# A hybrid decoder block on one core: within an attention head, the next head's maxima earlier and the head's own scores later

## The chip, the core and the metric

The kernel runs on one core of a Trainium2 chip. TensorE (PE) multiplies matrices and writes into PSUM; VectorE (DVE) and ScalarE (ACT) read PSUM and the on-chip memory SBUF; GpSimd (POOL) works on SBUF and issues some of the transfers; SyncE (SP) only issues transfers (DMA). Each engine runs its own queue of instructions in order and waits for others by semaphores. The metric is the device time of one execution in microseconds (us), as the median of several; lower is better.

## The reference

One decoder block over 1024 tokens of width 1024, all in float32. Two groups of eight attention heads read the same normalised input. Group B (forgetting attention) adds cumulated log forget gates as a bias; group A lets each query attend to the 256 keys that an indexer scores highest, with a linear distance bias (ALiBi). Then come an output projection and a mixture of 32 experts, of which each token uses two. What the change touches is the attention:

```python
def forgetting_attention(q, k, v, log_f):
    ...
        logits = jnp.einsum('bqhd,bshd->bhqs', qb, k).astype(jnp.float32) * scale
        logits = logits + jnp.transpose(cb, (0, 2, 1))[..., None] - cum_k[:, :, None, :]
        ...
        p = jax.nn.softmax(logits, axis=-1).astype(v.dtype)
        o = jnp.einsum('bhqs,bshd->bqhd', p, v)
...
def dsa_attention(q, k, v, iq, ik, iw):
    ...
        _, idx = lax.top_k(score, n_top)
        ...
        logits = logits - slopes[None, None, :, :, None] * dist[:, :, None, None, :]
        logits = jnp.where(valid[:, :, None, None, :], logits, -jnp.inf)
        p = jax.nn.softmax(logits, axis=-1).astype(v.dtype)
```

## The kernel before

The sixteen heads run one after the other in a loop (line 1091) of 17 stages. Heads 0 to 7 are group B, 8 to 15 group A. Stage n mixes the steps of three heads:

- **scores of head n** (`score_steps`): twelve blocks, for two halves of 512 queries and each block of 128 keys up to them. A block forms the product of keys and queries in PSUM (`pst`) in two parts (`kx` by `qx`, then `ky` by `qy`, the low-order parts) plus a third product for the mask (`diagT` in group B, `maskT` in group A). ACT takes the exponential into `P`.
- **values of head n-1** (`value_steps`): twelve products of `P` with the values, collected in `po`. Each is two matmul records in the trace.
- **maxima of head n+1** (`max_steps`): for eight blocks of 128 queries the row `qx` by `kx` is formed in `pmax`, and DVE takes the largest logit of each query into `mx`. Then `finish` turns `mx` on PE (`pmt`), ACT copies it negated into `mr`, and SP copies `mr` into a row of `qx` of head n+1, so that the scores come out with the maximum already taken off. The scores of head n+1 need that copy.

There are two sets of operand tiles `qx, kx, qy, ky`, for even and odd heads (in the order of the instructions their numbers are 2764 to 2767 for even heads and 2876 to 2879 for odd ones). `prep(n + 2)` reloads the set of head n for head n+2: SP copies the queries into `qx` (from `QB` or `QA`), clears the row of the maxima (`qx<-qx`), copies the keys into `kx` (from `KB`; for heads 8 and 9 from `KA`; for heads 10 to 15 they stay), then `qy` and `ky`; POOL copies the rows of the gates (`CU`) or the slopes (`sl`). All of these must wait until head n's last scores have read the set, and head n+2's maxima must wait for them.

What else runs in a stage comes from `side(n)`: the search for the 256th largest index score (stages 0 to 3), the masks (4 to 7), sums of the adaLN vectors (in stages 8, 10, 12 and 14 POOL loads eight tiles `wada` of 512 KB, and DVE adds them up), squares and their column sums for the norms (`osq`, `psqc`).

`merge` sets the order: each list of steps is spread over a stretch of the stage, from `lo` to `hi` as shares of the stage, in proportion to each step's cost, and single steps have a place of their own. The steps are then sorted by place and issued; PE keeps that order. A scheduler orders the other engines' queues by when it expects each instruction to be ready.

```python
            todo.append((lo + (hi - lo) * (t + 0.5 * c) / tot, k, f))
    ...
    for _, _, f in sorted(todo, key=lambda z: z[:2]):
```

Of the kernel before, what the change touches and what calls it, by code (L numbers as in the profile page):

```python
# [38 lines left out]
def hymba_block(ctx: ExitStack, tc: tile.TileContext, x, c, w_ada, b_ada, g_mix, w_in, b_forget,  # L39
# [13 lines left out]
    def u(name, dt=F32, shape=(128, 1024)):  # L53
        return upool.tile(list(shape), dt, name=name, tag="u", bufs=NU)
# [13 lines left out]
    def mm(*a, **k):  # L68
        i = tc.keep_in_program_order(T.matmul(*a, **k))  # L69
        at["pe"] = i  # L70
        return i
# [9 lines left out]
    def ps1(name, shape=(128, 512), dt=F32):  # L81
        return psum.tile(list(shape), dt, name=name, tag="p", bufs=4)
# [653 lines left out]
    def max_steps(n):  # L736
        par, masked = n % 2, n >= 8
        e = E0[par]
        mx = []

        def rows(i):
            if not mx:
                mx.append(sm("mx", [128, 8]))
            w_ = (i + 1) * 128
            p = ps2("pmax")
            plain = masked and i >= 2
            for n0 in range(0, w_, 512):
                m = min(512, w_ - n0)
                last = n0 + m == w_
                mm(p[:, n0:n0 + m], qx[par][:, i * 128:(i + 1) * 128], kx[par][:, n0:n0 + m],  # L750
                   start=True, stop=plain or not last)
                if last and not plain:
                    mm(p[:, i * 128:w_], identb, diag, start=False, stop=True)
            if plain:
                V.tensor_tensor_reduce(mjunk[:, :w_], p[:, :w_], madd[i], 1.0, NEG, OP.add, OP.max,  # L755
                                       accum_out=mx[0][:, i:i + 1])
            else:
                V.tensor_reduce(mx[0][:, i:i + 1], p[:, :w_], AX.X, OP.max)  # L758

        def finish():  # L760
            p = ps1("pmt2")
            tr(p[0:8, 0:128], mx[0], identf)
            mr = sm("mr", [8, 128], F32R, bufs=1)
            S.activation(mr, p[0:8, 0:128], AF.Copy, scale=-1.0)
            cp(qx[par][e + 4:e + 5], mr)

        return [((i + 1) * 0.11 + 0.2, lambda i=i: rows(i)) for i in range(NT)], finish

    def score_steps(n, P):

        par, masked = n % 2, n >= 8
        tl = {}

        def block(hf, kb):
            q0 = max(kb * 128, hf * 512)
            m = (hf + 1) * 512 - q0
            p = ps1("pst")
            free = not masked and q0 != kb * 128
            mm(p[:, :m], kx[par][:, kb * 128:(kb + 1) * 128], qx[par][:, q0:q0 + m], start=True, stop=False)
            mm(p[:, :m], ky[par][:, kb * 128:(kb + 1) * 128], qy[par][:, q0:q0 + m], start=False, stop=free)  # L780
            if masked:
                mm(p[:, :m], identb, maskT[kb][:, q0:q0 + m], start=False, stop=True)
            elif not free:
                mm(p[:, :128], identb, diagT, start=False, stop=True)
            if hf == 0:
                slot = (0, 0), (0, 512), (1, 0), (0, 896)
            else:
                slot = (0, 0), (0, 512), (1, 0), (1, 512), (2, 0), (2, 512), (3, 0), (2, 896)
            i, off = slot[kb]
            if (hf, i) not in tl:  # L790
                tl[hf, i] = u("P")
            P[hf, kb] = tl[hf, i][:, off:off + m], q0
            S.activation(P[hf, kb][0], p[:, :m], AF.Exp)  # L793

        return [((hf + 1) * 512 - max(kb * 128, hf * 512), lambda hf=hf, kb=kb: block(hf, kb))
                for hf in range(2) for kb in range(4 * hf + 4)]
# [8 lines left out]
    def value_steps(n, P):  # L805

        j, par = (n % 8) // 2, n % 2
        g, blk, h = (1, 1 + j, 2 * j + par) if n < 8 else (0, 0, j + 4 * par)
        z, row = h // 2, MAIN[h % 2]
        cols = slice(0, 128) if par == 0 else slice(64, 192)  # L810
        po = {}

        def step(hf, kb):
            if kb == 0:
                po[hf] = ps1("po")
                if (g, hf, z // 2) not in O:
                    O[g, hf, z // 2] = u(f"O{g}{hf}", shape=(128, 2, 512))
                if (g, z) not in DEN:
                    DEN[g, z] = u("den")
            pt, q0 = P[hf, kb]  # L820
            mm(po[hf][:, q0 - hf * 512:], vblock(blk, kb)[:, cols], pt, start=(kb == 0), stop=(kb == 4 * hf + 3))
            if kb == 4 * hf + 3:
                S.activation(DEN[g, z][row, hf * 512:(hf + 1) * 512], po[hf][OTHER[par]], AF.Copy)
                S.activation(otile(g, hf, z)[row], po[hf][MAIN[par]], AF.Copy)

        return [((hf + 1) * 512 - max(kb * 128, hf * 512), lambda hf=hf, kb=kb: step(hf, kb))
                for hf in range(2) for kb in range(4 * hf + 4)]

    def normalise(g, z):

        den = DEN[g, z]
        st = {}

        def guess():
            st["r"] = r = u("rden")
            paced(S.activation(r, den, AF.Ln))
            S.activation(r, r, AF.Exp, scale=-1.0)

        def one():
            paced(V.tensor_tensor(den, den, st["r"], op=OP.mult))  # L840

        def two():
            paced(V.scalar_tensor_tensor(st["r"], den, 2.0, st["r"], op0=OP.subtract, op1=OP.mult))

        def times(hf):
            o = otile(g, hf, z)
            paced(V.scalar_tensor_tensor(o, o, -1.0, st["r"][:, hf * 512:(hf + 1) * 512], op0=OP.mult, op1=OP.mult))

        return [guess, one, two, lambda: times(0), lambda: times(1)]
# [44 lines left out]
    def prep(n):  # L894

        j, par = (n % 8) // 2, n % 2
        e = E0[par]
        if n < 8:
            h = 2 * j + par
            fill_q(par, QB[j])  # L900
            fill_k(par, KB[j])
            cp(qx[par][e + 2:e + 3], CU[96 + h:97 + h], G)
            cp(qx[par][e + 3:e + 4], CU[64 + h:65 + h], G)
            cp(kx[par][e:e + 1], CU[32 + h:33 + h], G)
            cp(kx[par][e + 1:e + 2], CU[h:h + 1], G)
            fill_cross(par, QB[j], KB[j])
        else:
            if n < 10:
                fill_k(par, KA)
                paced(G.memset(kx[par][e:e + 2].bitcast(F32), 0.0))  # L910
                cp(kx[par][e + 2:e + 3], held["pos"][0:1], G)
            h = j + 4 * par
            sl = held["sl"]
            fill_q(par, QA[j])
            cp(qx[par][e + 2:e + 3], sl[h:h + 1], G)
            cp(qx[par][e + 3:e + 4], sl[32 + h:33 + h], G)
            fill_cross(par, QA[j], KA if n < 10 else None)
# [147 lines left out]
    for m in range(4):  # L1065
        if m == 2:
            rows, finish = max_steps(0)
            rows = [f for _, f in rows]
# [18 lines left out]
    if True:  # L1087
        PP = {}
        norm = []
        NW = (0.2, 0.66, 0.73, 0.8, 0.87)  # L1090
        for n in range(17):
            streams = []
            if n < 16:
                PP[n] = {}
                streams.append(((0.07, 0.65) if n else (0.25, 0.85), score_steps(n, PP[n])))
            if n:
                streams.append(((0, 1), value_steps(n - 1, PP[n - 1])))
            if n + 1 < 16:
                rows, finish = max_steps(n + 1)
                streams.append(((0.15, 0.65) if n else (0, 0.5), rows))  # L1100
            extra = side(n)
            if n + 1 < 16:
                extra.append((0.75, finish))
            if n + 2 < 16:
                extra.append((0.79 if n else 0.9, lambda n=n: prep(n + 2)))
            if norm:
                extra += zip(NW if n < 16 else (0.1, 0.2, 0.25, 0.3, 0.35), normalise(*norm.pop()))
            merge(streams, extra)
            if n and n <= 8 and (n - 1) % 2:
                norm.append((1, (n - 1) // 2))  # L1110
            if n - 1 in (10, 11, 14, 15):
                norm.append((0, {10: 0, 11: 2, 14: 1, 15: 3}[n - 1]))
        for f in normalise(*norm.pop()):
            f()
# [315 lines left out]
    for i in range(NT):  # L1430
# [11 lines left out]
        if i in (5, 7):  # L1442
            i0, n = {5: (0, 4), 7: (4, 2)}[i]
# [310 lines left out]
    with tc.If(most > 128):  # L1754
# [58 lines left out]
        rows = u("ovri", I32, (128, 2, 16))  # L1813
# [85 lines left out]
```

## Time and profile before

| | us |
|---|---|
| median of 3 runs (1204.28 to 1205.78) | 1204.99 |
| the profiled execution | 1199.19 |
| its span, first to last instruction | 1197.2 |
| PE busy (88% of the span) | 1055.7 |
| DVE busy (77%) | 919.0 |
| ACT busy (56%) | 670.0 |
| POOL busy (25%) | 300.3 |

The heads stand between some 362 and 697 us of the span. Times of instructions and waits are of the profiled execution, 5.8 us below the median. A matmul's recorded end is modelled, and the next one may start before it; a wait is the idle time of the engine ahead of an instruction, put down to the semaphore that came last.

### The profile page before, as it was taken

How to read it: one execution, taken by the hardware profiler on the slowest of the kernel's cores; microseconds unless marked ns; L12 is line 12 of the kernel's file. 1: busy time of each engine (PE TensorE's matmuls, PEld its weight loads, DVE VectorE, ACT ScalarE, POOL GpSimd, SP SyncE). 2: the span in 40 equal slices, each digit the busy share in tenths (PEclk: the TensorE clock that was granted, in tenths of full speed). 3: DMA queues.
4: the chain of work that ended last, by engine and by line, in shares of the span. 5: the costliest groups of instructions: out<-in, count | busy, mean ns of one | idle time of the engine just before them, and what ended most of it. 6: DMA issues, size and time to landing. Idle time of an engine off the chain costs nothing.

```text
span 1197.2 us, 15378 instructions
## 1 busy us (share of the span) xinstructions
PE 1055.7 (88%) x4983; PEld 796.5 (67%) x4983; DVE 919.0 (77%) x1785; ACT 670.0 (56%) x1177; POOL 300.3 (25%) x253
## 2 busy tenths in 40 slices
PE   2789999699988998998989999975999999889881
PEld 2678899588865555654656678864777777666650
DVE  5946568899976589566578665795999999888847
ACT  7544666764546545654554622334777777656635
POOL 0341031212040110213212212551222222333223
PEclk9699999899998999999999999986999999999986
DMA  8510102243463433556336634776999999999946
GB/s 345 164 36 1 41 20 65 106 150 114 149 169 89 108 81 81 133 142 195 115 87 198 245 123 141 247 251 216 311 342 320 308 314 308 317 317 315 321 117 247
DMA packets 91414, 219.94 MB, mean 184 GB/s; under 512 B 30516, under 2 KB 40932, under 8 KB 91328
## 3 DMA queue, kind: packets, MB, share of 16 engines
q1 hardware_dynamic: 75776, 185.23, 46.5%
q0 software_dynamic: 15552, 33.66, 10.3%
q8 instruction: 42, 0.69, 0.2%
q14 instruction: 44, 0.36, 0.1%
HBM read 192.43 MB, written 42.99 MB: 197 GB/s over the span
## 4 chain that ended last, share of the span: by engine, by line
PE 49%; DVE 24%; DMA 16%; ACT 5%; issue 3%; SPq 1%; POOL 1%; DVEq 0%; ACTq 0%; POOLq 0%
PE pgu L69 10%; PE py L69 6%; PE pst L69 6%; DVE mjunk L460 6%; PE po L69 6%; PE pout L69 5%; DMA raw<-in_w_gate_dram 4%; DMA raw<-in_w_down_dram 4%; PE pp L285 3%; PE pmax L69 3%; PE pvv L407 2%; DMA qx<-mr 2%; PE pxt L74 2%; ACT sjunk L464 1%; DMA raw<-in_w_up_dram 1%
## 5 line engine op out<-in xcount | busy, mean ns | idle before, releaser
L69 PE MATMUL po<-P,VT 128*128 128x512 f32 (+3 forms) x384 | 148.3, 499 | 0.3 <-ACT P L793 0.3
L793 ACT ACTIVATE P<-pst 128x512 f32<-128x512 f32 x192 | 90.9, 489 | 95.1 <-PE pst L69 93.2
L1570 POOL DMA_INDIRECT x2d<-y,tab x31 | 59.3, 1912 | 204.9 <-DVE wgu1l L1492 46.1
L69 PE MATMUL pst<-qx,kx 128*128 128x512 f32 x192 | 94.3, 491 | 13.3 <-DMA qx<-mr 11.2
L758 DVE TENSOR_REDUCE mx<-pmax 128x1 f32<-128x128 f32 (+3 forms) x80 | 52.7, 674 | 44.6 <-PE pmax L69 44.2
L69 PE MATMUL py<-raw,af 128*128 128x512 f32 x128 | 69.2, 623 | 14.3 <-DMA raw<-in_w_down_dram 14.3
L69 PEld LDWEIGHTS po<-P,VT 128*128 128x128 f32 x384 | 66.1, 195 | 18.0 <-issue 9.8
L69 PE MATMUL pmax<-kx,qx 128*128 128x512 f32 (+1 forms) x192 | 68.1, 420 | 6.4 <-DMA kx<-KB 2.0
L69 PE MATMUL py<-wd0h,ahl 128*128 128x512 f32 x128 | 67.9, 530 | 2.4 <-ACT wd0h L1491 1.9
L69 PE MATMUL pst<-qy,ky 128*128 128x512 f32 x192 | 67.6, 352 | 0.0
L358 DVE SCALAR_TENSOR_TENSOR score<-relu,iw,score 128x384 f32<-128x384 f32 (+5 forms) x42 | 43.1, 1026 | 26.7 <-ACT relu L353 23.7
L69 PEld LDWEIGHTS pst<-qx,kx 128*128 128x128 f32 x192 | 37.9, 197 | 34.2 <-issue 20.8
L285 PE MATMUL pp<-hh,wbh 128*128 128x512 f32 x128 | 51.2, 400 | 9.3 <-DVE pjl L634 9.3
L755 DVE CUSTOM_DVE_ANT_0 mjunk<-pmax,madd 128x384 bf16<-128x384 f32 (+5 forms) x48 | 42.6, 888 | 20.6 <-PE pmax L69 20.5
L69 PE MATMUL pout<-woh,oh 128*128 128x512 f32 x128 | 52.2, 408 | 2.4 <-DVE ssq L871 2.4
L460 DVE TENSOR_SCALAR_CACHE_REDUCE mjunk<-k,low 128x768 bf16<-128x768 uint16 (+1 forms) x64 | 51.8, 810 | 1.5
L1482 POOL DMA_INDIRECT xg<-h2d,tab x32 | 39.0, 1218 | 49.6 <-PE pxt L74 35.2
L1492 DVE TENSOR_TENSOR wgu2l<-raw,wgu2h 128x512 fp32r<-128x512 f32 x64 | 43.8, 685 | 9.7 <-ACT wgu2h L1491 9.6
L285 PE MATMUL pp<-hl,wbh 128*128 128x512 f32 x128 | 50.9, 398 | 0.0
L69 PE MATMUL pout<-woh,ol 128*128 128x512 f32 x128 | 50.8, 397 | 0.0
L285 PE MATMUL pp<-hh,wbl 128*128 128x512 f32 x128 | 50.8, 397 | 0.0
L69 PE MATMUL pout<-wol,oh 128*128 128x512 f32 x128 | 50.4, 394 | 0.0
(430 smaller groups left out, 3263.1 us busy)
## 6 DMA issues: line engine op xcount, KB each, us to landing
raw<-in_w_gate_dram SPq DMA_DIRECT2D x64, 512.0 KB
raw<-in_w_up_dram SPq DMA_DIRECT2D x64, 512.0 KB
raw<-in_w_down_dram SPq DMA_DIRECT2D x64, 512.0 KB
wada<-in_w_ada_dram POOLq DMA_DIRECT2D x32, 512.0 KB, 5.5
x<-in_x_dram SPq DMA_DIRECT2D x16, 512.0 KB
wada<-in_w_ada_dram SPq DMA_DIRECT2D x16, 512.0 KB
wbr<-in_w_in_dram SPq DMA_DIRECT2D x8, 512.0 KB
qy<-QB SPq DMA_DIRECT2D x16, 256.0 KB
```

The lines of the kernel that those rows point to most:

```text
L69: i = tc.keep_in_program_order(T.matmul(*a, **k))
L74: i = tc.keep_in_program_order(T.transpose(*a))
L285: at["mm"] = T.matmul(p[:, :n], w(k, a), hT[b][k][:, n0:n0 + n], start=(i == 0), stop=(i == 23))
L358: last = V.scalar_tensor_tensor(score[i], r, wv, score[i], op0=OP.mult, op1=OP.add)
L407: at["mm"] = T.matmul(p[:, :ng], hT[a][k][:, t * 128:(t + 1) * 128], parts[k // kk][b][:, k % kk, :], start=(i == 0), stop=(i == 23))
L460: paced(V.tensor_scalar(mjunk[:, :(i + 1) * 128], src, thr, None, op0=op, op1=OP.add, accum_out=self.col(self.cnt, i)))
L755: V.tensor_tensor_reduce(mjunk[:, :w_], p[:, :w_], madd[i], 1.0, NEG, OP.add, OP.max, accum_out=mx[0][:, i:i + 1])
L758: V.tensor_reduce(mx[0][:, i:i + 1], p[:, :w_], AX.X, OP.max)
L793: S.activation(P[hf, kb][0], p[:, :m], AF.Exp)
L1482: return ko(G.indirect_dma_start(out=XG[e], out_offset=None, in_=h2d, in_offset=bass.IndirectOffsetOnAxis(ap=tab[:, e:e + 1], axis=0), bou ...
L1492: ko(V.tensor_tensor(lo, w, hi.bitcast(F32), op=OP.subtract))
L1570: return G.indirect_dma_start(out=x2d, out_offset=bass.IndirectOffsetOnAxis(ap=at_, axis=0), in_=y, in_offset=None, bounds_check=L - 1, oo ...
```

## The change

Three places in the loop over stages. The scores of a stage go from 0.07 to 0.65 of it to 0.17 to 0.76; the next head's maxima from 0.15 to 0.65 to 0.09 to 0.58; their transposition and transfer from 0.75 to 0.68. Stage 0 keeps its places, and `prep` stays at 0.79 everywhere.

```diff
             if n < 16:
                 PP[n] = {}
-                streams.append(((0.07, 0.65) if n else (0.25, 0.85), score_steps(n, PP[n])))
+                streams.append(((0.17, 0.76) if n else (0.25, 0.85), score_steps(n, PP[n])))
             if n:
                 streams.append(((0, 1), value_steps(n - 1, PP[n - 1])))
             if n + 1 < 16:
                 rows, finish = max_steps(n + 1)
-                streams.append(((0.15, 0.65) if n else (0, 0.5), rows))
+                streams.append(((0.09, 0.58) if n else (0, 0.5), rows))
             extra = side(n)
             if n + 1 < 16:
-                extra.append((0.75, finish))
+                extra.append((0.68 if n else 0.75, finish))
             if n + 2 < 16:
                 extra.append((0.79 if n else 0.9, lambda n=n: prep(n + 2)))
```

PE at the boundary from head 2 to head 3, before: the last score block of head 2, a value step, the transposition of head 3's maxima, five value steps, and head 3's first scores.

```order
L69 MATMUL pst<-qx_2764,kx_2765 128x128
L69 MATMUL pst<-qy_2766,ky_2767 128x128
L69 LDWEIGHTS identb
L69 MATMUL pst<-diagT,identb 128x128
L69 MATMUL po<-P,VT_647 128x512
L74 MATMUL pmt_3407<-identf,mx 8x128
L69 MATMUL po<-P,VT_647 128x512
L69 MATMUL po<-P,VT_647 128x384
L69 MATMUL po<-P,VT_647 128x256
L69 MATMUL po<-P,VT_649 128x128
L69 MATMUL po<-P,VT_649 128x512
L69 MATMUL pst<-qx_2876,kx_2877 128x512
```

PE there now: the last of the three score blocks of head 2 that follow the transposition of head 3's maxima, five value steps, and the first maxima product of head 4.

```order
L69 MATMUL pst<-qx_2764,kx_2765 128x128
L69 MATMUL pst<-qy_2766,ky_2767 128x128
L69 LDWEIGHTS identb
L69 MATMUL pst<-diagT,identb 128x128
L69 MATMUL po<-P,VT_647 128x512
L69 MATMUL po<-P,VT_647 128x384
L69 MATMUL po<-P,VT_647 128x256
L69 MATMUL po<-P,VT_649 128x128
L69 MATMUL po<-P,VT_649 128x512
L69 MATMUL pmax<-kx_2765,qx_2764 128x128
L69 LDWEIGHTS identb
L69 MATMUL pmax<-diag,identb 128x128
```

The transposition moved ahead of the last three score blocks, and head 4's first maxima, which read the reloaded set 2764 and 2765, took the place of head 3's first scores behind the five value steps.

SP at the end of that head, before: the reload of the even set for head 4 (`QB_2135` and `KB_2328` are where its queries and keys come from) begins ahead of the copy of head 3's maxima into the odd set.

```order
L718 DMA qx_2764<-QB_2135 64x1024
L718 DMA qx_2876<-mr 1x8x128
L718 DMA qx_2764<-qx_2764 1x16x64
L718 DMA kx_2765<-KB_2328 64x1024
L718 DMA qy_2766<-QB_2135 64x1024 x2
```

SP there now.

```order
L718 DMA qx_2876<-mr 1x8x128
L718 DMA qx_2764<-QB_2135 64x1024
L718 DMA qx_2764<-qx_2764 1x16x64
L718 DMA kx_2765<-KB_2328 64x1024
L718 DMA qy_2766<-QB_2135 64x1024 x2
```

The copy of the maxima now leads, and the four reloads follow each other. At the end of head 0 the order is as it was: the reload of `qx` for head 2 first, then the copy of head 1's maxima.

POOL in stage 8, where the slope rows of head 10 stand between loads for the adaLN sums, before.

```order
L718 DMA qx_2876<-sl 1x16x64 x2
L1036 DMA wada<-in_w_ada_dram 128x1024 x5
L718 DMA qx_2764<-sl 1x16x64
L1036 DMA wada<-in_w_ada_dram 128x1024 x2
L718 DMA qx_2764<-sl 1x16x64
L1036 DMA wada<-in_w_ada_dram 128x1024
```

POOL there now.

```order
L718 DMA qx_2876<-sl 1x16x64 x2
L1036 DMA wada<-in_w_ada_dram 128x1024 x6
L718 DMA qx_2764<-sl 1x16x64
L1036 DMA wada<-in_w_ada_dram 128x1024
L718 DMA qx_2764<-sl 1x16x64
L1036 DMA wada<-in_w_ada_dram 128x1024
```

One load moved ahead of the first slope row. In stages 10 and 12 the rows of heads 12 and 14 stand as here: a row, a load, a row.

## Rows read from the trace of the kernel before

**Rows 1.** The stretch of the heads: length, then busy us (instructions) by engine, clock.

```profile
core 0: us, PE busy (x) PEld busy (x) DVE busy (x) ACT busy (x) POOL busy (x), PEclk, DMA share, GB/s
361.72:653.21 291.49, 267.16 (x1227) 167.00 (x1226) 205.70 (x361) 154.50 (x305) 54.41 (x91) 0.98 0.45 122
```

**Rows 2.** PE's waits from 369 to 660 us: total us, times, longest.

```profile
PE pst L69 <- DMA qx<-mr: 11.2, 8, 2.9
PE pmt L74 <- DVE mx L758: 2.6, 2, 1.4
PE pmt L74 <- DVE mx L755: 2.3, 2, 1.5
PE pmax L69 <- DMA kx<-KB: 2.0, 4, 0.6
PE pst L69 <- ACT osq L863: 1.4, 1, 1.4
PE pmax L69 <- DVE mx L758: 1.3, 3, 0.8
```

**Rows 3.** Timeline, end of head 2: start, length, engine, what, [wait <- releaser].

```profile
405.59 0.31 PE L69 MATMUL pst<-qx,kx 128*128 128x128 f32 x1
...
405.91 1.08 PE L69 MATMUL po<-P,VT 128*128 128x512 f32 x2
...
405.93 0.44 SPq L718 DMA_DIRECT2D qx<-QB  x1
...
408.35 0.27 PE L74 MATMUL pmt<-identf,mx 128*8 128x128 f32 x1 [1.36 <-DVE mx L758]
...
408.46 3.18 PE L69 MATMUL po<-P,VT 128*128 128x512 f32 x10
...
408.95 0.69 SPq L718 DMA_DIRECT2D qx<-mr  x1
409.68 0.54 SPq L718 DMA_DIRECT2D qx<-qx  x1
410.27 0.58 SPq L718 DMA_DIRECT2D kx<-KB  x1
...
413.93 0.30 PE L69 MATMUL pmax<-kx,qx 128*128 128x128 f32 x1 [0.64 <-DMA kx<-KB]
```

**Rows 4.** Timeline, end of head 1: the reload of kx and its reader.

```profile
391.22 0.58 SPq L718 DMA_DIRECT2D kx<-KB  x1
...
395.31 0.30 PE L69 MATMUL pmax<-kx,qx 128*128 128x128 f32 x1 [0.59 <-DMA kx<-KB]
```

**Rows 5.** Timeline, end of head 0.

```profile
369.06 1.13 PE L69 MATMUL po<-P,VT 128*128 128x512 f32 x2
...
370.95 0.58 SPq L718 DMA_DIRECT2D kx<-KB  x1
...
373.10 0.76 PE L69 MATMUL pst<-qx,kx 128*128 128x512 f32 x1 [2.91 <-DMA qx<-mr]
```

**Rows 6.** Timeline, end of head 8: slope row, adaLN load, head 9's first scores.

```profile
516.65 0.30 PE L69 MATMUL pst<-qx,kx 128*128 128x128 f32 x1
...
517.25 0.50 POOL L718 DMA_DIRECT2D qx<-sl  x1 [13.07 <-PE pst L69]
517.75 0.55 POOL L1036 DMA_DIRECT2D wada<-in_w_ada_dram  x1
...
523.74 0.47 PE L69 MATMUL pst<-qx,kx 128*128 128x512 f32 x1 [2.31 <-DMA qx<-mr]
```

**Rows 7.** Transfers into qx whose landing is recorded, from issue to landing.

```profile
DMA to landing us min/median/max: 2.9/3.5/5.1
```

**Rows 8.** Timeline, end of stage 11: the column sums.

```profile
586.00 1.84 PE L69 MATMUL psqc<-ones,osq 128*128 128x1 f32 x16
```

**Rows 9.** Busy time and granted clock of three stretches, columns as in rows 1.

```profile
372.50:379.30 6.80, 6.20 (x21) 4.43 (x21) 2.67 (x11) 1.47 (x3) 0.00 (x0) 0.50 0.83 189
466.05:484.50 18.45, 17.27 (x80) 10.38 (x78) 18.29 (x29) 8.77 (x18) 3.49 (x8) 1.00 0.40 89
608.00:611.40 3.40, 3.40 (x11) 1.98 (x9) 1.28 (x1) 1.59 (x3) 0.00 (x0) 0.51 0.83 181
```

## The prediction

> **What bounds the kernel now.** I first took the busy time of the whole stretch of heads, then the list of what TensorE (PE) waited for in it, then the timeline of single boundaries between two heads. In the 291.49 us from the first scores of head 0 to those of head 15, PE works 267.16 us; VectorE (DVE) works 205.70 and ScalarE (ACT) 154.50 [rows 1]. PE runs its instructions in the order of the code, so the time is PE's work plus what it waits for, and a reordering can only change the waits. The list names them [rows 2]: 11.2 us in 8 waits of a head's first scores for the copy of its negated maxima (qx<-mr), 2.6 + 2.3 us of the transposition of the maxima (pmt) for the last maximum on DVE, 2.0 us of the first maxima product (pmax) for the reload of kx, 1.4 us for an ACT queue that is blocked by osq, 1.3 us of pmax for DVE.
>
> The timeline of the boundary from head 2 to head 3 shows why [rows 3]. The last scores of head 2 start at 405.59. They free qx and kx, so SP issues the reload for head 4 at 405.93. PE goes on with a value step (1.08 us), waits 1.36 us for the maximum and transposes at 408.35. The copy of mr is issued at 408.95, and only behind it, in SP's order, come qx<-qx (409.68) and kx<-KB (410.27). PE covers all this with five value steps, 3.18 us long, and two score blocks; at 413.93 pmax of head 4 still waits 0.64 us for kx. So two chains end at PE after every head: maxima, mr, first scores; and last scores, reload, first maxima.
>
> **The change part by part.** *What goes.* PE's order now is: pmt, three score blocks, five value steps, two maxima, value, maximum, and only then the next head's first scores. From pmt to those scores there are then at least 3.18 us of values plus three score blocks and four products; the mr copy was waited for at most 2.9 us beyond the 3.18 us of values. I take all 11.2 us as gone. Before pmt there now stand two 512-wide score blocks and a value step where two narrow blocks and a value step stood, and a further value step; the added step alone is 1.08 us [rows 3], against waits of 1.4 and 1.5 us at most: I take the 4.9 us as gone, too. The 2.0 us for kx are replaced by what follows. Sum: 18.1 us.
>
> *What comes.* The reload still waits for the head's last scores, but the next maxima come sooner after them. Cover: from the last scores' start to the next step 0.32 us (405.59 to 405.91), then the five value steps, 3.18 us: 3.50 us. Chain: 0.34 us to the first issue, two issues of 0.44 and 0.54 us with their gaps of about 0.05 (kx comes 0.59 after qx<-qx), so kx is issued 1.42 us after the last scores, since mr no longer stands between. From the issue of kx to the maxima that it released it took 3.66 us (410.27 to 413.93) [rows 3] and 4.09 (391.22 to 395.31) [rows 4]; I take 3.9. So the maxima can start 5.3 us after the last scores, and PE waits 5.3 - 3.5 = **1.8 us** (1.6 to 2.0) for each of heads 3 to 9, whose kx is reloaded: 12.6 us.
>
> Head 2 stands apart: at the end of head 0 SP's order is not changed, and in PE's order only one value step stands between the last scores and head 2's maxima. That step ends at 369.06 + 1.13 = 370.19; kx is issued at 370.95 and lets the maxima start at 374.85: **4.7 us**, where PE waited 2.91 for mr before (counted above) [rows 5].
>
> Heads 10 to 15 keep kx; their last piece is the second slope row (qx<-sl) on POOL's queue. Into heads 10, 12 and 14 the change puts one adaLN load (wada) between the two rows, where two stood at head 10. First row 0.60 us after the last scores, row 0.50, load 0.55 [rows 6], landing 3.5 us after its issue (median; 2.9 to 5.1) [rows 7]: 5.15 us, less 3.5: **1.65 us**, three times 5.0. Into heads 11, 13 and 15 no load stands between: 0.60 + 0.50 + 3.5 = 4.6, a wait of **1.1 us**, but head 13's maxima stand behind sixteen column sums of 1.84 us [rows 8] that cover it: 2.2 us. New waits in all: 4.7 + 12.6 + 5.0 + 2.2 = **24.5 us**.
>
> *What the new waits give back.* While PE stands, ACT and DVE catch up: the osq wait and DVE's 1.3 us before pmax lie just behind the new wait, and I count them as absorbed, 2.7 us (0 to 2.7). The granted clock was 0.50 (1.2 GHz) in two stretches [rows 9]: for 6.8 us after the 2.91 us wait at head 1, and for 3.4 us from 608.0, where PE worked throughout. The second costs 1.7 us and goes, if no wait as long as those before it follows; in the first PE worked 6.20 us at half clock, lost 3.1, and would start 1.75 us later, losing 2.2. Together 2.6 us.
>
> *Sum:* -18.1 - 2.7 - 2.6 + 24.5 = **+1.1 us**. The profiled execution took 1199.19 us (span 1197.2 and 2 us around it), 5.8 below the median of the runs, 1204.99; I add the difference to the median: **1206.1 us**, +0.1%. Under 0.2% (2.4 us) no measurement of this kernel tells a difference from no change. Its own range: with 3.66, 2.9 and 2.9 us for the three landings it is 4.7 us less, 1201.4; with 4.09 us for kx (+1.3), nothing absorbed (+2.7) and one half-clock stretch more (+1.7) it is 1212, of which I take 1211.
>
> The Trainium skill ("DMA: Bandwidth & Descriptors", Anatomy of one DMA) gives a transfer some 2.0 us fixed and then 436 GB/s, for GpSimd's path; by an estimate from that page the 256 KB of kx would land in 2.6 us, the wait of heads 3 to 9 would be 0.5 us, and the sum -8.0 us. It speaks for the faster rival; the rows above, 3.66 and 4.09 us to the released product, speak against it.
>
> **The rivals.** *The reload lands sooner.* Part of the 3.66 to 4.09 us might be due to the mr copy and to packets around it, which move away. The fastest landing of a qx transfer is 2.9 us [rows 7]. A landing 1.0 us shorter for kx and 0.6 us for the slope rows takes 1.0 + 7.0 + 1.8 + 1.2 = 11.0 us off: **1195 us**. Against it: both rows of kx agree within 0.5 us, and behind the first-issued 256 KB a second one can't start at once.
>
> *The adaLN loads hold the reload up.* At heads 10, 12 and 14 the slope rows and qx<-qx share the transfer engines with 512 KB loads that POOL issues in between. At head 9 the 4 KB of mr, issued behind two such loads, were what PE waited for until 523.74, 2.31 us [rows 6]. If the second slope row takes the 5.1 us of the slowest [rows 7], those three waits are 3.25 us, above the 2.91 us that half clock followed: +4.8 us and, with a stretch of 3.4 us at half clock for each, +5.1: **1211 to 1216 us**, slower. It decides from a wait of some 2.5 us on.
> The skill says on the same page (Issuing engines are not separate DMA queues) that all queues run on the same sixteen engines and interleave; head 9's row agrees in direction.
>
> *DVE stays the one waited for.* In head 6 DVE is busy 18.29 of 18.45 us [rows 9], as it builds the masks. If its backlog moves along, the 4.9 us at pmt and the 2.7 us absorbed come back: all of it +7.6 us, 1213.7; half of it **1210 us**. Against it: the added cover before pmt is over 1 us, and DVE's mask work needs nothing of PE, so it runs on in the new wait.
>
> **How the numbers follow.** The forecast has 0.45 (same 0.33, faster 0.05, slower 0.07), the sooner reload 0.20 (faster), the adaLN loads 0.20 (slower), DVE 0.15 (slower 0.10, same 0.05). So faster 0.25, same 0.38, slower 0.37. Range 1196 to 1214: what lies beyond is half of the first rival and half of the second.
>
> **What would show it.** In the profile of the changed kernel: pst waits for qx<-mr near 0; pmt waits for DVE near 0; pmax waits for kx<-KB, 4.7 us once and 1.6 to 2.0 in heads 3 to 9, and for qx<-sl or qx<-qx of 1 to 2 us later; SP's kx issue 1.4 us behind the last scores; one stretch at 0.50 of the clock. Waits of pmax under 1 us would be the first rival, over 2.9 us at heads 10, 12, 14 the second, pmax or pmt waiting for DVE the third. It is wrong altogether if PE's work itself, 267 us, changes.

## The result and the profile after

The changed kernel takes 1239.62 us (median of 4 runs, 1239.42 to 1244.88) beside 1205.38 us for the kernel before (4 runs, 1204.28 to 1209.19): a ratio of 1.0297 [1.0260, 1.0334], slower by 3%. The forecast was 1206.1 us, within 1196 to 1214. The profiled execution took 1239.42 us with a span of 1237.7, 40.5 us over the span before. The medians lie only 34.2 us apart: the profiled execution before was some 6 us below its median and the one after at its own, so the stretches below overstate the loss by about these 6 us in all.

The stretch of the heads comes first (length, busy time by engine, granted clock, as in [rows 1]):

```profile
362.48:687.02 324.54, 277.87 (x1219) 173.89 (x1228) 209.22 (x361) 153.47 (x305) 54.95 (x91) 0.94 0.41 109
```

It is 33.05 us longer. PE's busy time rose from 267.16 to 277.87 us for nearly the same products (1219 records instead of 1227), so 10.71 us are PE's own and 22.3 are idle time. The next view says what PE waited for between 362 and 700 us (total, times, longest), to be read beside [rows 2]:

```profile
PE pmax L69 <- DMA qx<-sl: 20.6, 5, 7.5
PE pmax L69 <- DMA kx<-KB: 11.6, 4, 4.7
PE pmax L69 <- DMA kx<-CU: 5.1, 2, 2.7
PE pmax L69 <- DVE mx L758: 2.7, 2, 1.7
PE pmax L69 <- DVE mx L755: 2.2, 3, 1.0
PE pmax L69 <- DMA qx<-qx: 2.1, 2, 1.1
...
PE pmt L74 <- DVE mx L758: 0.6, 1, 0.6
```

The 11.2 us for the mr copy are gone, and so are the 4.9 us of pmt: the 0.6 us shown stands at head 1's maxima, ahead of the window of [rows 2], and stood there before as well. In their place the first maxima wait for the reload, 20.6 + 11.6 + 5.1 + 2.1 = 39.4 us. The timeline of the same boundary as in [rows 3], end of head 2, shows how:

```profile
411.19 0.69 SPq L718 DMA_DIRECT2D qx<-mr  x1
...
411.46 0.31 PE L69 MATMUL pst<-qx,kx 128*128 128x128 f32 x1
...
411.79 3.24 PE L69 MATMUL po<-P,VT 128*128 128x512 f32 x10
411.98 0.45 SPq L718 DMA_DIRECT2D qx<-QB  x1
...
412.48 0.67 SPq L718 DMA_DIRECT2D qx<-qx  x1
...
413.20 0.58 SPq L718 DMA_DIRECT2D kx<-KB  x1
...
417.31 0.30 PE L69 MATMUL pmax<-kx,qx 128*128 128x128 f32 x1 [2.28 <-DMA kx<-KB]
```

The last scores start at 411.46, the value steps cover PE until 411.79 + 3.24 = 415.03, and the maxima start 5.85 us after the scores that free their operands.

Where the 40.5 us lie is read from stretches with the same ends in both kernels: from head 1's first scores to head 8's, from there to head 15's, and from the first output projection product (pout) to the end. Before:

```profile
373.10:504.12 131.02, 122.66 (x566) 75.72 (x567) 94.04 (x168) 71.39 (x141) 20.22 (x39) 0.98 0.39 89
504.12:653.21 149.09, 136.59 (x617) 86.14 (x618) 101.37 (x168) 75.78 (x147) 32.28 (x49) 0.99 0.52 154
676.12:1197.18 521.06, 453.27 (x2127) 349.99 (x2125) 423.86 (x804) 288.60 (x502) 159.51 (x89) 0.94 0.79 266
```

After:

```profile
378.53:526.08 147.55, 128.33 (x568) 78.48 (x568) 95.48 (x170) 70.03 (x141) 20.58 (x40) 0.93 0.34 77
526.08:687.02 160.94, 138.78 (x604) 88.47 (x613) 103.87 (x166) 76.12 (x147) 32.46 (x47) 0.96 0.48 139
709.81:1237.66 527.85, 458.47 (x2127) 354.05 (x2125) 420.82 (x804) 291.05 (x504) 155.71 (x89) 0.92 0.79 263
```

They are 16.5, 11.9 and 6.8 us longer; head 0 adds 4.7, and 0.8 lie ahead of it. In each stretch the granted clock is lower. The clock rows of single stretches, of the profile after:

```profile
373.30:380.10 6.80, 4.20 (x12) 2.69 (x13) 3.51 (x9) 0.20 (x1) 0.00 (x0) 0.50 0.87 195
...
417.60:421.00 3.40, 3.40 (x12) 1.89 (x11) 1.27 (x3) 0.00 (x0) 0.00 (x0) 0.51 0.84 182
...
sum 40.80, PE 35.21 PEld 22.31 DVE 22.70 ACT 4.21 POOL 0.00; mean PE 3.91 PEld 2.48 DVE 2.52 ACT 0.47 POOL 0.00
```

The last line sums all nine stretches at half clock (1.2 GHz) between 370 and 700 us. Each begins during or right behind a wait of the first maxima. Before there were 10.2 us of it in two stretches [rows 9]. PE was busy for 35.21 us at half clock where it had been for 9.60, and half of the difference, 12.8 us, is about what its busy time grew by.

### The profile page after: what moved, and what is told of

Read it like the earlier page. It is cut to its first block, busy times and chain, and to the rows that moved or that the text cites. A ratio compares the mean times of both kernels' runs of the same rounds, so it can differ in the third digit from the quotient of the medians.

```text
span 1237.7 us, 15345 instructions
## 1 busy us (share of the span) xinstructions
PE 1069.6 (86%) x4973; PEld 805.2 (65%) x4983; DVE 918.1 (74%) x1785; ACT 669.2 (54%) x1177; POOL 297.0 (24%) x253
## 4 chain that ended last, share of the span: by engine, by line
PE 47%; DVE 20%; DMA 17%; issue 8%; ACT 4%; POOL 2%; SPq 1%; DVEq 0%; POOLq 0%; ACTq 0%
PE pgu L69 9%; DVE mjunk L460 6%; PE py L69 6%; PE po L69 6%; PE pout L69 5%; PE pst L69 5%; DMA raw<-in_w_down_dram 5%; PE pp L285 3%; DMA wada<-in_w_ada_dram 3%; PE pmax L69 3%; DMA raw<-in_w_gate_dram 3%; PE pvv L407 2%; DMA raw<-in_w_up_dram 2%; PE pxt L74 1%; DMA qx<-sl 1%
## 5 line engine op out<-in xcount | busy, mean ns | idle before, releaser
L793 ACT ACTIVATE P<-pst 128x512 f32<-128x512 f32 x192 | 88.1, 489 | 133.6 <-PE pst L69 93.3
L69 PE MATMUL po<-P,VT 128*128 128x512 f32 (+3 forms) x384 | 156.7, 521 | 1.1 <-issue 0.6
L69 PE MATMUL pmax<-kx,qx 128*128 128x512 f32 (+1 forms) x192 | 77.7, 471 | 46.3 <-DMA qx<-sl 20.6
L1570 POOL DMA_INDIRECT x2d<-y,tab x31 | 56.8, 1832 | 208.1 <-DVE at L1538 53.5
L69 PEld LDWEIGHTS pmax<-kx,qx 128*128 128x128 f32 x192 | 38.2, 210 | 71.2 <-issue 56.4
L69 PEld LDWEIGHTS po<-P,VT 128*128 128x128 f32 x384 | 68.8, 205 | 16.8 <-issue 9.8
L150 DVE SCALAR_TENSOR_TENSOR acc<-wada,cs,acc 128x1024 f32<-128x1024 f32 x28 | 41.4, 1479 | 15.8 <-DMA wada<-in_w_ada_dram 15.6
```

Of the source, the lines that this page charges most:

```text
L150: return V.scalar_tensor_tensor(acc, w, cs[:, j:j + 1], acc, op0=OP.mult, op1=OP.add)
L1570: return G.indirect_dma_start(out=x2d, out_offset=bass.IndirectOffsetOnAxis(ap=at_, axis=0), in_=y, in_offset=None, bounds_check=L - 1, oo ...
```

## The experiments

**Theory and rivals.** The theory: the reload of an operand set can't start before the last scores have read it and is needed by the next first maxima; the change brings these two nearer, from both sides, and the half clock that follows most of these waits makes them dearer. Rivals: the maxima put nearer to the begin cost by themselves (PSUM, DVE); the adaLN loads on POOL's queue, or DVE's sums of them, set the masked heads' pace; half clock is hidden.

**Only the scores moved.**

```diff
-streams.append(((0.07, 0.65) if n else (0.25, 0.85), score_steps(n, PP[n])))
+streams.append(((0.17, 0.76) if n else (0.25, 0.85), score_steps(n, PP[n])))
```

> Only the scores are moved (0.17 to 0.76); maxima and finish stay as before. By the order, a FoX head's first maxima now stand 6 po blocks behind the last scores of the head whose operand set they take (after: 5; before: 6 po and 3 to 6 scores of the next head). Theory (the reload of the operand set, which the last scores release, is late for the first maxima): the wait at the first maxima comes back, 1.4 to 1.9 us in each of heads 3 to 9 and 1.5 to 7 us in heads 8 to 15 where slope rows come last; pst<-qx on mr stays gone; the time is 1218 to 1232 us. Rival (it is the maxima put nearer to the begin, with PSUM and DVE behind them, that cost): the first maxima wait under 0.5 us in heads 3 to 9 and the time is 1200 to 1208 us.

Measured: 1234.83 us, 1.0230 [1.0191, 1.0269]. PE's waits in the heads:

```profile
PE pmax L69 <- DMA kx<-KB: 14.3, 6, 4.0
PE pmax L69 <- DMA qx<-qx: 11.2, 5, 3.5
PE pmax L69 <- DMA qx<-sl: 3.5, 2, 1.8
```

The mr wait is gone and the reload's is there, 2.0 to 2.2 us in heads 3 to 7; wait and time both come out a little over the theory's ranges. The later scores alone bring most of the loss.

**Only the maxima moved.**

```diff
-streams.append(((0.15, 0.65) if n else (0, 0.5), rows))
+streams.append(((0.09, 0.58) if n else (0, 0.5), rows))
...
-extra.append((0.75, finish))
+extra.append((0.68 if n else 0.75, finish))
```

> Only the maxima (0.09 to 0.58) and their finish (0.68) are moved; the scores stay as before. By the order three scores of the next head still stand between the five po blocks and the first maxima, and these wait for the mr row as before. Theory (the reload): the wait for mr at the next head's first scores stays at about 1.6 us a head and covers the reload, so the first maxima wait under 0.7 us in heads 3 to 9; the time is 1199 to 1211 us. Rival (the earlier maxima are the cause): the first maxima wait 2 us or more, or DVE holds them, and the time is 1222 us or more.

Measured: 1223.77 us, 1.0136 [1.0097, 1.0175]: a time within the rival's range, and a miss for mine. The timeline at the end of head 2 shows what I had left out:

```profile
408.05 0.30 PE L69 MATMUL pst<-qx,kx 128*128 128x128 f32 x1
...
408.39 0.44 SPq L718 DMA_DIRECT2D qx<-QB  x1
...
410.37 0.70 SPq L718 DMA_DIRECT2D qx<-mr  x1
...
411.70 0.58 SPq L718 DMA_DIRECT2D kx<-KB  x1
...
412.74 0.55 PE L69 MATMUL pst<-qx,kx 128*128 128x512 f32 x1
...
415.61 0.30 PE L69 MATMUL pmax<-kx,qx 128*128 128x128 f32 x1 [2.02 <-DMA kx<-KB]
```

The finish at 0.68 ends the mr wait at 412.74 by itself, and with it goes the cover of the reload. SP has the mr copy between qx<-QB and the rest, so kx is issued 3.65 us after the last scores, and the maxima wait 1.6 to 2.1 us in heads 3 to 7, mostly between the two expectations. It is the reload again, not PSUM or DVE. From head 1 to head 8 PE's idle time grows by 4.6 us (12.98 against 8.36) and the stretch by 10.8 (141.77 against 131.02), at a clock of 0.92 instead of 0.98. From head 8 to head 15 it takes 164.90 us, 15.8 more than before and 4.0 more than in the changed kernel, at a clock of 0.91: there the mr waits stay (12.3 us in five) and 5.2 us for the reload come on top. Why this part is longer than in the changed kernel was not tried. Taken together, the two halves' 2.3 and 1.4% are more than the whole's 3.0%; each alone brings the reload's wait.

**The wait filled with work of PE**, in the changed kernel.

```diff
 p = ps2("pmax")
+if i == 0 and n >= 2:
+    for _ in range(40):
+        mm(p[:, 512:640], identb, identb, start=True, stop=True)
```

> The changed kernel with 40 products of identb by identb (128 columns each, into columns 512 to 640 of pmax, which nothing reads) before the first maxima of heads 2 to 15: about 2.1 us of work for PE inside the wait. Nothing of the result changes. Theory (the wait lets the clock fall to half in the stretch behind it, and that costs time of its own): the half-clock stretches in the heads shrink from about 41 us to under 15 us; 12 us of that come back, against some 4 us that the filling itself costs in heads 11, 13 and 15, whose wait is shorter than it; 1226 to 1234 us. Rival (only the waits cost, and half clock behind them is hidden): 1239 to 1246 us, since the filling is extra work where the wait is short.

Measured: 1232.25 us, 1.0211 [1.0177, 1.0246], inside the theory's range. From head 1's first scores to head 8's:

```profile
376.98:517.72 140.74, 134.82 (x848) 89.47 (x848) 96.20 (x170) 70.09 (x141) 21.03 (x40) 1.00 0.36 83
```

PE executes 280 more products there, the clock is 1.00 instead of 0.93, and the stretch is 6.8 us shorter. So the half clock behind a wait does cost. Some 22 us of it are left from head 0 to head 15, where the changed kernel has 41 and under 15 were expected: 13.7 us in the masked heads, where PE still stands 2.2 us ahead of head 10's maxima and 5.6 us ahead of head 12's, the rest around head 0. From head 8 to head 15 the filled kernel takes 163.98 us, 3.0 more than the changed one, so the gain lies in the forgetting heads.

**The same filling where only the maxima moved** (the edit of the run before, on that kernel).

> The kernel with only the maxima moved (1223.8 us, half clock for about 41 us more than before in the heads), with 40 products of identb by identb before the first maxima of heads 2 to 15, as in the run with the filled wait. Theory (a wait of about 1.7 to 2.1 us in each head lets the clock fall, and that costs as much again): half clock in heads 3 to 8 goes, the heads' periods there fall from 20.2 us to 18.5 to 19.2 us; 1208 to 1217 us in all. Rival (half clock is hidden behind other waits): the periods stay within 0.3 us and the time is 1222 to 1232 us.

Measured: 1223.52 us, 1.0162 [1.0117, 1.0207]; without the filling it was 1223.77. The periods of heads 3 to 7, each from the first scores of the head before to its own, fall about as the theory has it, to 18.7 to 19.6 us from 20.0 to 20.6 (head 8's grows from 19.9 to 20.9), the clock from head 1 to head 8 is 1.00, and that stretch shrinks from 141.77 to 135.79 us. The masked heads gain 1.9 us. The profiled span falls by 6.7 us, but the profiled execution was here the lowest of its four runs (1219.60 us) and without the filling the highest (1226.25). The median does not fall and lies in the rival's range: the price of half clock shows in the stretch and is not shown in the whole time.

**The slope rows on SP**, in the changed kernel.

```diff
-cp(qx[par][e + 2:e + 3], sl[h:h + 1], G)
-cp(qx[par][e + 3:e + 4], sl[32 + h:33 + h], G)
+cp(qx[par][e + 2:e + 3], sl[h:h + 1])
+cp(qx[par][e + 3:e + 4], sl[32 + h:33 + h])
```

> The changed kernel with the two slope rows qx<-sl of heads 8 to 15 issued on SP instead of POOL, so that they no longer stand between the adaLN loads on POOL's queue. Theory (the queue makes them late): the waits of 5.0, 7.5 and 2.1 us before the first maxima of heads 10, 12 and 14 become 1.5 to 2.8 us each (SP issues them 1.3 us behind qx<-qx), one or two half-clock stretches fewer; 1228 to 1235 us. Rival (the loads hold the DMA engines, on whichever queue the rows stand): the waits of heads 10 and 12 stay over 4 us and the time is 1237 to 1243 us.

In the changed kernel head 12's boundary stands like this (timeline; the wada rows are the 512 KB loads):

```profile
583.66 0.57 POOL L1036 DMA_DIRECT2D wada<-in_w_ada_dram  x1
...
584.22 0.50 POOL L718 DMA_DIRECT2D qx<-sl  x1
...
584.71 0.55 POOL L1036 DMA_DIRECT2D wada<-in_w_ada_dram  x1
585.25 0.50 POOL L718 DMA_DIRECT2D qx<-sl  x1
...
593.89 0.45 PE L69 MATMUL pmax<-kx,qx 128*128 128x128 f32 x1 [7.45 <-DMA qx<-sl]
```

The second slope row, of a few KB, releases PE 8.6 us after its issue; [rows 7] had 5.1 us at most. With the rows on SP the time is 1245.62 us, 1.0320 [1.0280, 1.0360], above both ranges. The waits of heads 10, 12 and 14 fall to 1.7, 4.7 and 1.0 us, but those of heads 9, 11 and 13 rise to 4.1, 2.5 and 3.6 us, and in sum (from 515 us on, heads 9 to 15) they are what they were, 19.7 us in the changed kernel:

```profile
PE pmax L69 <- DMA qx<-sl: 19.5, 7, 4.7
```

Head 12 in this run:

```profile
582.80 1.21 SPq L718 DMA_DIRECT2D qx<-sl  x2
...
589.44 0.44 PE L69 MATMUL pmax<-kx,qx 128*128 128x128 f32 x1 [4.69 <-DMA qx<-sl]
```

The second row (issued some 0.6 us behind the first) still takes 6 us from its issue, with no load ahead of it on its queue: both theories are half right. The Trainium skill ("DMA: Bandwidth & Descriptors", Issuing engines are not separate DMA queues) has all queues share the same sixteen engines; this run agrees, 4.7 us at head 12 where the queue of the loads gave 7.5.

**Fewer adaLN loads**, in the changed kernel.

```diff
-w = u("wada")
-paced(G.dma_start(w, ...))
-ada_add(acc, w, j)
+if j == 0:
+    held["w"] = u("wada")
+    paced(G.dma_start(held["w"], ...))
+ada_add(acc, held["w"], j)
```

> The changed kernel with one adaLN block loaded in each of stages 8, 10, 12 and 14 instead of eight; the sums use that one block eight times, so the result is another one, and 7 loads of 512 KB a stage are left out. DVE's work stays. Theory (the loads hold up the slope rows of heads 10, 12 and 14, on the queue or on the DMA engines): their waits of 5.0, 7.5 and 2.1 us fall to 1.0 to 2.5 us each, with one or two half-clock stretches fewer; 1226 to 1234 us. Rival (DVE's sums, not the loads, make stages 8 to 15 late): the waits stay and the time is 1237 us or more.

Measured: 1240.35 us, 1.0294 [1.0244, 1.0343]: the waits as the theory has them, the time as the rival has it. PE's waits from 526 to 700 us:

```profile
PE pmax L69 <- DMA qx<-qx: 6.3, 5, 1.5
PE pmax L69 <- DVE mx L755: 6.3, 6, 1.7
PE pmt L74 <- DVE mx L755: 3.6, 2, 2.8
PE pmax L69 <- DVE mx L758: 1.7, 1, 1.7
```

With seven of eight loads away no head from 10 on waits over 1.5 us for its rows, so the loads did hold them up. But DVE is now late for 11.6 us, where it was for 3.9 in the same stretch of the changed kernel; from head 8 to head 15 it takes 157.16 us instead of 160.94, and the stretch from pout on is longer by as much (531.83 against 527.85 us, clock 0.92 in both). So the slope rows' waits alone do not set the time there: DVE stands right behind them.

**Four operand sets.** Heads take `qx` and `kx` from four sets in turn, and their rows are loaded at 0.3 of the stage instead of 0.79, so the reload no longer waits for the scores of the stage; `cross` is the part of `prep` that loads `qy` and `ky`.

```diff
-par, masked = n % 2, n >= 8
+par, masked, s4 = n % 2, n >= 8, n % 4
...
-mm(p[:, n0:n0 + m], qx[par][:, i * 128:(i + 1) * 128], kx[par][:, n0:n0 + m],
+mm(p[:, n0:n0 + m], qx[s4][:, i * 128:(i + 1) * 128], kx[s4][:, n0:n0 + m],
...
-extra.append((0.79 if n else 0.9, lambda n=n: prep(n + 2)))
+extra.append((0.3 if n else 0.1, lambda n=n: prep(n + 2)))
+extra.append((0.79 if n else 0.9, lambda n=n: cross(n + 2)))
```

> The changed kernel with four sets of the operand tiles qx and kx, taken in turn by n mod 4, so that a head's rows are loaded at 0.3 of the stage two ahead of it, into a set whose last scores lie a stage back; the rows of qy and ky stay at 0.79. Theory (the waits before the first maxima are the reload that the last scores release): these waits, 39 us in the changed kernel, fall under 6 us, half clock in the heads under 17 us, and what the change took out (the wait for the mr row) stays out; 1184 to 1200 us. Rival (something else is as late: PSUM, DVE or the adaLN loads): waits of another name take their place, over 15 us in sum, and the time is 1206 us or more.

> The kernel before with the same four sets and early loads. By its order the wait for the mr row at the next head's first scores covers the reload, so the sets should buy little: the waits for mr stay at about 11 us, the time is 1198 to 1209 us. If it is as fast as the changed kernel with four sets (within 3 us), the change itself is worth nothing once the reload is out of the way.

Measured: 1210.98 us, 1.0052 [1.0027, 1.0077], with the change; 1204.15 us, 0.9992 [0.9959, 1.0025], without it. No first maxima wait for a transfer any more. With the change, head 1 to head 8 and head 8 to head 15:

```profile
374.19:498.12 123.93, 119.06 (x567) 74.05 (x567) 96.08 (x172) 70.00 (x141) 19.23 (x37) 0.99 0.44 99
498.12:664.59 166.47, 146.35 (x613) 92.83 (x613) 100.78 (x166) 76.49 (x147) 32.52 (x47) 0.91 0.47 136
```

and PE's longest waits in the second:

```profile
PE prow L69 <- DVE acc L1048: 8.9, 2, 4.5
PE pmax L69 <- DVE mx L760: 5.9, 3, 2.2
PE plc L69 <- issue: 3.4, 1, 3.4
```

In the forgetting heads the theory holds: 147.55 us became 123.93, 7 us less than before the change. In the masked heads, and in the time, the rival does: the column sum of the adaLN block (prow) now waits for DVE's adaLN sums, the clock is 0.91, and the stretch is the longest of all kernels here. Without the change it is 158.72 us, the mr waits grow (14.2 us in the heads, against 11.2), and the gain of the forgetting heads is lost again; head 1 to head 8 there:

```profile
376.08:502.15 126.07, 118.92 (x567) 73.30 (x567) 95.84 (x173) 71.33 (x141) 20.23 (x38) 1.00 0.43 103
```

So on four sets throughout the change still costs 6.8 us between the medians: it gains 2.1 us in the forgetting heads, over the same 567 products, and loses 7.8 us in the masked heads and 6.5 us from pout on (527.05 against 520.60).

**The change in one half of the heads at a time** (the conditions `if n` become `0 < n < 7`, or `n >= 7`; elsewhere the numbers of before).

> The change in stages 1 to 6 alone (the forgetting heads); stages 7 to 15 as before. If the parts are independent: from head 1's first scores to head 8's 145 to 149 us (changed kernel 147.5, before 131.0), from head 8's to head 15's 147 to 153 us as before (149.1), the wait for ssq at the out projection 2 to 3 us as before; 1221 to 1231 us. Rival (what the forgetting heads lose is made up later, or pushes the masked heads into new waits): the masked heads leave that range.

> The change in stages 7 to 15 alone (the masked heads); stages 1 to 6 as before. If independent: head 1 to head 8 about 131 us, head 8 to head 15 158 to 163 us (changed kernel 160.9), the wait for ssq at the out projection 5 to 7 us with more half clock behind it, so that from the first pout to the end it takes 4 to 7 us more than before (521.1); 1218 to 1227 us. Rival (the lengthening behind the heads has nothing to do with stage 15's later scores): the wait for ssq stays at 2 to 3 us and the stretch behind within 2 us of 521.

Measured: 1221.09 us, 1.0107 [1.0079, 1.0134], for the forgetting heads; 1231.15 us, 1.0212 [1.0189, 1.0235], for the masked ones. The two add up to 1.0319, about the whole change. In the first, heads 2 to 7 wait 4.62, 2.49, 2.29, 2.31, 2.75 and 2.52 us for the reload, as in the changed kernel; head 1 to head 8 takes only 139.82 us, below the expected range, since stage 7 keeps its old places and head 7's first scores come 14.6 us behind head 6's (21.4 in the changed kernel). Head 8 to head 15 takes 154.01, a little over, at a clock of 0.97. In the second, head 8 to head 15 takes 160.10 us, as expected, but head 1 to head 8 takes 137.39 instead of 131, since its stage 7 has the change, and the time lies over its range. The wait for ssq at pout is 2.4 us in the first and 5.8 us in the second, and the stretch from pout on is 3.5 and 8.1 us longer than before. A single such stretch is uncertain by some 5 us, but all profiles say the same: it takes 520.6 to 525.7 us in the seven kernels whose last scores keep their places, 527.1 to 531.8 in the seven where they are moved. The lengthening does come from the last head's later scores.

**Four sets for the forgetting heads alone**, with and without the change in stages 1 to 6.

```diff
-par, masked = n % 2, n >= 8
+par, masked, s4 = n % 2, n >= 8, n % 4 if n < 8 else n % 2
...
-extra.append((0.79 if n else 0.9, lambda n=n: prep(n + 2)))
+extra.append(((0.3 if n < 6 else 0.79) if n else 0.1, lambda n=n: prep(n + 2)))
```

> The kernel before with four sets of qx and kx for the forgetting heads alone (rows loaded at 0.3 of the stage two ahead), the masked heads with two sets and their loads as before. Expected from the run with four sets throughout on the kernel before: head 1 to head 8 about 126 us (before 131.0), head 8 to head 15 147 to 153 us; 1195 to 1203 us. Rival (the gain is lost again in the masked heads): head 8 to head 15 takes 154 us or more, 1203 to 1208 us.

> The same with the change put back in stages 1 to 6: what the change is worth once the reload is out of the way, in the heads where DVE is not late. Theory: head 1 to head 8 about 124 us against 126 without it, the rest alike, so 1193 to 1202 us, 1 to 3 us under the run without it. Rival (the wait for the mr row was covered by other work, so that its removal is worth nothing): within 1 us of it.

Measured: 1203.05 us, 0.9977 [0.9953, 1.0000], without the change, at the edge of what was expected, since head 8 to head 15 takes 156.00 us (the rival's mark was 154); 1193.75 us, 0.9902 [0.9875, 0.9929], with it, so this kernel beats the one without the change and the one before. Head 1 to head 8 and head 8 to head 15, with the change:

```profile
371.17:494.34 123.17, 116.15 (x560) 71.80 (x560) 95.74 (x171) 70.15 (x141) 16.69 (x31) 1.00 0.50 118
494.34:648.71 154.37, 139.16 (x617) 87.63 (x618) 100.69 (x167) 75.65 (x146) 32.05 (x48) 0.97 0.43 128
```

Head 1 to head 8 without the change:

```profile
373.94:502.79 128.85, 120.34 (x567) 74.09 (x567) 96.55 (x173) 71.45 (x141) 16.50 (x31) 0.99 0.45 113
```

So the change is worth something, where nothing it moves nearer is waited for. That it is 9.3 us and not the 1 to 3 expected is only half explained. The profiled execution without the change was the longest of its twelve (1209.46 us). Of the 15.0 us between the two profiled spans, 6.6 lie behind head 8's first scores and 1.9 ahead of head 0's, where the edit moves no step, with a lower clock in the one without the change (0.92 against 0.94 from pout on). Of the 5.7 us between the two stretches, a part is their ends: with the change head 1's scores are moved and head 8's are not, so 560 products stand where 567 do without it. What of the 9.3 us the change itself is worth stays open; the two kernels with four sets throughout, over equal products, have 2.1 us in these heads.

## Why the prediction was wrong

| step of the prediction | said, us | measured, us |
|---|---|---|
| waits for mr and at pmt that go (and the 2.0 for kx, replaced below) | -18.1 | -18.1 |
| osq and DVE before pmax, absorbed | -2.7 | +2.2 |
| new wait, head 2 | 4.7 | 4.7 |
| new waits, heads 3 to 9 | 12.6 | 17.9 |
| new waits, heads 10, 12, 14 | 5.0 | 14.6 |
| new waits, heads 11, 13, 15 | 2.2 | 2.1 |
| the clock | -2.6 | +10.7 |
| behind the heads | 0 | +6.8 |

The mechanism was the one forecast: what was said to go has gone, the reload is what PE waits for, and head 2's wait was right to a tenth. Four terms failed, and the absorbed one turned its sign. The measured column, taken from the profiled executions, sums to 40.9 us; the spans differ by 40.5 and the medians by 34.2.

With them failed the premise that a reordering can only change the waits. PE's own work rose from 267.16 to 277.87 us, which the prediction had named as the sign that it is wrong altogether: 35.21 us of it ran at half clock, where 9.60 did before.

*Heads 3 to 9, 1.8 us each.* At the end of head 2 the cover was 3.57 us (3.50 said), the chain 5.85 (5.3 said). I had written that mr no longer stands between. It does no longer stand between qx<-QB and qx<-qx, but its issue starts at 411.19, just ahead of the last scores, and holds SP until 411.88; with a slower qx<-qx (0.67 against 0.54) kx is issued after 1.74 us instead of 1.42, and its way to the reader took 4.11 instead of 3.9. Five such heads wait 2.2 to 2.7 us. Heads 8 and 9 wait 3.0, and it is a slope row that releases them, where the sum went by kx. The estimate from the Trainium skill's page ("DMA: Bandwidth & Descriptors", Anatomy of one DMA), a wait of 0.5 us here, is farther off still; the measurement decides.

*Heads 10, 12 and 14.* The wait was worked out with the median landing of a row, 3.5 us, and the rival's ceiling with the slowest, 5.1 us. Behind the 512 KB loads it took 8.6 us at head 12, and the three waits were 5.0, 7.5 and 2.1 us. The rival had the right mechanism at too low a price. Taking the loads away gains nothing in time, though: DVE is waited for instead. Heads 11, 13 and 15 came out right in sum partly by luck: at heads 11 and 15 it was qx<-qx that released the maxima, not the slope row that the sum went by.

*Absorbed.* The osq wait went, but DVE's waits before pmax rose from 1.3 to 4.9 us, 1.05 of them in stage 5, one of those in which it builds the masks, and 3.9 behind head 8's first scores. That is the kind of wait that the third rival named; why it grew was not taken apart.

*The clock.* This is the largest miss, 13.3 us. I took from two rows before (2.91 us followed by half clock, 2.31 not) that waits under some 2.5 us are free of it. The changed kernel's 2.28 us at 417.31 were followed by half clock, the 3.00 us at 524.75 and head 7's 2.31 us at 480.27 were not:

```profile
480.27:483.67 3.40, 3.40 (x18) 2.03 (x19) 3.37 (x8) 0.60 (x1) 0.00 (x0) 1.00 0.97 216
524.75:528.15 3.40, 3.33 (x17) 2.54 (x18) 1.66 (x4) 0.60 (x1) 0.00 (x0) 1.00 1.03 266
```

and in the kernel with only the maxima moved a wait of 1.56 us at 395.08 was. Before, too, the 2.42 us that end at 699.70, behind the stretch that I had read, were followed by it (0.50 from 700.20 to 703.60). The length of one wait does not decide it in these traces. What these kernels have in common is that such a wait recurs in every forgetting head; that this is the cause was not shown, and head 7's wait speaks against it as the whole of it. The filled wait showed that the half clock is a cost, the four sets that it goes with the waits: from head 1 to head 8 PE is busy 119.06 us at a mean clock of 0.99 and 128.33 at 0.93.

*Behind the heads.* I ended the sum at head 15. The scores of the last head come later in its stage as well, so the norm behind it does, and the out projection waits for ssq (before, then after):

```profile
699.70 0.50 PE L69 MATMUL pout<-woh,oh 128*128 128x512 f32 x1 [2.42 <-DVE ssq L871]
```

```profile
738.02 0.80 PE L69 MATMUL pout<-woh,oh 128*128 128x512 f32 x1 [5.86 <-DVE ssq L871]
```

That is 3.4 us more. In all, PE is idle 1.6 us longer from pout on and busy 5.2 us longer, at a clock of 0.92 instead of 0.94. The run with the change in the masked heads alone shows the longer wait again (5.8 us), the one in the forgetting heads alone doesn't (2.4). Which wait lowered the clock there later on was not tried.

The chances were off in one way: slower had 0.37, the highest single rival 1216. The rivals were priced one at a time, while dearer waits, half clock and the late end all came with the moved scores, at once.

## What to carry to other kernels

When steps are moved, look at the pair "last reader of a buffer, first reader of its next contents" and count what PE has between them now, and what stands in the queue that the reload passes. If the chain is longer, another set of buffers comes first and the reordering second: the same change costs 3% on two sets and was part of a gain of 1% where the forgetting heads alone had four sets and the new order. On four sets in all heads it still cost 0.6%, in heads where DVE was behind, so it is worth making only where no other wait stands right behind the one removed. A wait that recurs in every turn of a loop is to be priced with the half clock that may follow it, not at its length. And end the sum where the moved work is last waited for, not where the loop ends.

## What the hardware showed unexpectedly

In these traces half clock followed a wait of 1.56 us and stayed away after one of 3.00 us. A slope row of a few KB that shares the transfer engines with 512 KB loads released its reader 8.6 us after its issue on POOL, and 6 us after it on SP.
